# Decays of a gated recurrence as running products of f instead of exponentials of summed logarithms, in a two-layer float32 trunk on one core

## The chip, the cores and the metric

The kernel runs on one core of a Trainium2 chip. A core has a matrix engine (TensorE, PE in the profile, with PEld for its loading of stationary operands), a vector engine (VectorE, DVE), a scalar engine (ScalarE, ACT), GpSimd (POOL) and SyncE (SP), which here only issues transfers. Each engine works through its own queue in order and waits there for semaphores of the others. The metric is the device time of one execution in microseconds (us), as a median over runs.

## The reference

```python
for l in range(DEPTH):                                   # two layers, 256 tokens, width 1024, all float32
    x = x + 0.5 * swiglu(rms_norm(x, ffn1_norm[l]), ffn1_w_gate[l], ffn1_w_up[l], ffn1_w_down[l])
    h = rms_norm(x, mix_norm[l])
    if l < N_A_LAYERS:                                   # layer 0: gated linear recurrence, 6 heads of 128
        f = lb[l] + (1.0 - lb[l]) * sigmoid(f_raw)       # f_raw, q_raw, i_raw, g_raw: columns of h @ w_in_a
        q = silu(q_raw)
        o = hgrn2_recurrence(q, 1.0 - f, i_raw, log(f))  # S_t = diag(f_t) S_{t-1} + k_t v_t^T, o_t = S_t^T q_t
        main = rms_norm(o, hgrn_o_gain[l]) * silu(g_raw)
    else:                                                # layer 1: forgetting attention, 12 heads of 64
        main = forgetting_attention(q, k_sh, v_sh, cum_log_f) * sigmoid(gate)
    x = x + concatenate([main, memory_attention(...)]) @ w_out[l]
    x = x + 0.5 * swiglu(rms_norm(x, ffn2_norm[l]), ffn2_w_gate[l], ffn2_w_up[l], ffn2_w_down[l])
```

In the recurrence the score of query t against key s (s not after t) is the sum over 128 channels of q[t] k[s] times the product of f over the tokens after s up to t.

## The kernel before

**Weights and projections.** All weights stream from memory as 341 pieces of 128x1024. For each, ACT rounds the piece to a short float32 form (`wh`, line 359) and DVE forms the rest (`wl = raw - wh`, line 360); activations are split the same way into `xh` and `xl`. A product is three matmuls, wh*xh, wh*xl and wl*xh, each 128x128 by 256 columns, in a helper at line 294. Such matmuls are called dense here. Five pieces have room, so ACT and DVE can work up to five ahead of PE. A projection chunk is two pieces, 48 dense matmuls.

**Order.** PE runs in the order in which the program issues to it. A small planner, `Flow`, decides that order while the program is built: the dense matmuls advance a planned clock, and side work stands in generators (chains) that `yield` either a planned delay from the table `DELAY` or a condition. After every third dense matmul the planner lets one chain that is ready by the planned clock go on. Nothing on the chip follows these delays: if the data are late, PE waits at that place in its queue. The other engines' queues are ordered by a scheduler.

**PSUM.** The eight banks are `mm` (3, dense results), `lb` (2, scores and logits), `tb` (2, transposes) and `ob` (1, products with v).

**Mixer of layer 0.** `ORDER_A` gives the order of 15 chunks after the first FFN: f, q, i, g are the projections of three pairs of heads each, M the keys and values of the memory tokens, m the memory query. A chunk of f comes out with tokens on partitions; ACT takes the sigmoid, DVE applies the lower bound (rows `lv`, `ov`, spread over the partitions by two matmuls in `constants`) and clamps, PE transposes f to channels on partitions (12 transposes), and DVE forms k = 1 - f. `recurrence` then takes logarithms, splits them, and `decays` gets all products of f by matmuls of 512 columns with a constant 0/1 matrix `amat`: 8 for each of 6 heads, each pair of which ends in an exponential on ACT (line 929). There are seven levels (block lengths 64, 32, 16, 8, 4, 2, 1) and one slot for the step from the first 128 tokens to the second. `level_products` multiplies them by q or k, 128 columns at a time, on DVE and partly on POOL (lines 941, 944). `scores(hg)` multiplies per level on PE and copies the masked parts into a `unit` tile with predicated copies on DVE (line 971). `hgrn_out(hg)` multiplies by v into the one `ob` bank, squares on ACT (line 1031), forms 1/sqrt on DVE with eleven small instructions (lines 425 to 430), waits for the gate chunk g, multiplies (line 1041), transposes on PE after a planned delay `o0`, `o1` or `o2`, and `put` splits the result into the operand of the output projection (lines 665, 666).

**Elsewhere.** The memory attention of layer 0 starts when the scores of pair `MEM_WHEN` exist. `pair_out` is the product with v of the memory attention and of layer 1's attention (`fox_pair`, six pairs); it takes `ob` as soon as it is free, divides on DVE (lines 683, 691) and transposes. The output projection `project_out` takes four groups of rows in a given order, and finishes the chains of a group before it.

Of the kernel before, what the change touches and what calls it, by code (L numbers as in the profile page):

```python
# [27 lines left out]
TINY = 2.0 ** -62  # L28
# [5 lines left out]
         "f": 4.5, "ln": 7.5, "x": 7.5, "x2": 2.4, "norm_k": 8.2, "norm_b": 7.0, "norm_q": 8.75,  # L34
# [3 lines left out]
         "o0": 2.4, "o1": 1.42, "o2": 6.4, "mh": 1.0, "mp": 0.5, "cc": 74.5}  # L38
# [7 lines left out]
MEM_WHEN = 2  # L46
MEM_PRIO = 2
ORDER_A = "fffqMqqmiMiiggg"
# [46 lines left out]
def _stream(a):  # L95
# [4 lines left out]
    chunks = {"f": _as(wa[:, 768:1536]), "q": _ws(wa[:, 0:768]), "m": _as(wa[:, 3072:3328]),  # L100
# [21 lines left out]
def _shape_consts():  # L122

    u = np.arange(P)[:, None]
    t = np.arange(P)[None, :]

    def level(m):
        base = (t // (2 * m)) * (2 * m) + m
        up = (t % (2 * m)) >= m
        return np.where(up, (u >= base) & (u <= t), (u > t) & (u < base))  # L130

    suffix = u > t
    prefix = u <= t
    a = [level(m) for m in LEVELS]
    blocks = [a[0:4], a[4:7] + [suffix], a[4:7] + [prefix]]
    amat = np.concatenate([np.concatenate(b, axis=1) for b in blocks], axis=1).astype(np.float32)
    masks = np.zeros((P, len(LEVELS), 64), np.float32)
    for i, m in enumerate(LEVELS):
        s = np.arange(P)
        blk, low = s // (2 * m), (s % (2 * m)) < m  # L140
        cb = np.repeat(np.arange(64 // m), m)
        masks[:, i, :] = (blk[:, None] == cb[None, :]) & low[:, None]
    neg = np.where(np.arange(P)[None, :] > np.arange(P)[:, None], -1e30, 0.0).astype(np.float32)
    return amat, masks, neg, np.eye(P, dtype=np.float32)
# [6 lines left out]
def _layout(a):  # L151
    amat, masks, neg, ident = _shape_consts()
# [14 lines left out]
        "amat": amat,  # L167
# [72 lines left out]
def trunk(ctx: ExitStack, tc: tile.TileContext, d: dict, out: bass.AP):  # L240
# [8 lines left out]

    live = {"mm": 0, "lb": 0, "ob": 0, "hid": 0, "b6": 0}  # L250
# [9 lines left out]
    def free(tag, n=1):  # L260
        live[tag] -= n

    def has(tag, n=1):
        return lambda: live[tag] + n <= room[tag]

# [403 lines left out]
    def pair_out(pTs, v, heads, terms, mixed, k, gate=None, before=None):  # L669
        yield has("ob")  # L670
# [154 lines left out]
    con = {}  # L825

    lc = sb.tile([P, 12], F32, tag="lc", name="lc")
# [11 lines left out]
    def constants():  # L839
        yield lambda: softmax_c.done  # L840
        raw, araw = b6(), b6()
        with tc.issue_after(last_load[0]):
            for name, c, n in (("masks", 0, NM), ("wf", NM, KT * 12)):
                nc.sync.dma_start(out=raw[:, c:c + n], in_=d[name])
            nc.sync.dma_start(out=neg[:, P:T], in_=d["neg"])
            nc.sync.dma_start(out=fbias, in_=d["fbias"])
            nc.sync.dma_start(out=araw[:, 0:1536], in_=d["amat"])
# [5 lines left out]
        amat = con["amat"] = b6(F32R)  # L853
        G.tensor_copy(out=amat[:, 0:1536], in_=araw[:, 0:1536])
        free("b6", 2)

        G.tensor_tensor(out=lc[:, 6:12], in0=lc[:, 0:6], in1=lc[:, 0:6], op=ALU.subtract)
        lbt, lbd = b6(), b6()
        lv, ov = con["lv"], con["ov"] = lbt[:, 0:MAIN], lbt[:, MAIN:2 * MAIN]
        G.tensor_tensor(out=lbd[:, 0:MAIN].rearrange("p (h c) -> p h c", h=6),  # L860
                        in0=ident.unsqueeze(1).broadcast_to([P, 6, P]),
                        in1=lc[:, 6:12].unsqueeze(2).broadcast_to([P, 6, P]), op=ALU.mult)
        yield DELAY["const"]
        for i in range(2):
            b = bank("tb")
            mm(b[:, 0:384], ones, lbd[:, i * 384:(i + 1) * 384], True, True)
            S.copy(out=lv[:, i * 384:(i + 1) * 384], in_=b[:, 0:384])
        G.tensor_scalar(out=ov, in0=lv, scalar1=-1.0, scalar2=1.0, op0=ALU.mult, op1=ALU.add)
        free("b6")
# [10 lines left out]
    lv, ov = con["lv"], con["ov"]  # L880
# [3 lines left out]
    f, t1, t2, kT = b6(), b6(), b6(), b6()  # L884
    fv, t1v, t2v = tv(f), tv(t1), tv(t2)

    def f_chunk(c, o):
        yield lambda: st1.r is not None
        sl = slice(c * T, (c + 1) * T)
        for tt in range(2):  # L890
            S.activation(out=fv[:, tt, sl], in_=o[:, tt * T:(tt + 1) * T], func=AF.Sigmoid, scale=st1.r[:, tt:tt + 1])
        free("mm")
        fs = fv[:, :, sl]
        V.tensor_tensor(out=fs, in0=fs, in1=ov[:, sl].unsqueeze(1).broadcast_to([P, 2, T]), op=ALU.mult)
        V.tensor_tensor(out=fs, in0=fs, in1=lv[:, sl].unsqueeze(1).broadcast_to([P, 2, T]), op=ALU.add)
        V.tensor_scalar(out=t1v[:, :, sl], in0=fs, scalar1=TINY, scalar2=None, op0=ALU.max)
        V.tensor_scalar(out=t2v[:, :, sl], in0=fs, scalar1=1.0 / TINY, scalar2=TINY, op0=ALU.mult, op1=ALU.max)
        if c == 2:
            free("b6")
        yield DELAY["f"]  # L900
        b = bank("tb")
        for hh in range(2):
            for tt in range(2):
                transpose(b[:, (2 * hh + tt) * P:(2 * hh + tt + 1) * P], fv[:, tt, (2 * c + hh) * P:(2 * c + hh + 1) * P])
        V.tensor_scalar(out=kT[:, c * 512:(c + 1) * 512], in0=b, scalar1=-1.0, scalar2=1.0,
                        op0=ALU.mult, op1=ALU.add)
        if c == 2:
            free("b6")
# [4 lines left out]
    got = {"q": False, "x": set(), "s": set(), "v": set(), "g": set()}  # L913
    ss = [None] * 3
    box = con

    def decays(hg):

        for h in (2 * hg, 2 * hg + 1):
            e = [hid(), hid()]  # L920
            es[h] = [t.rearrange("p (t l c) -> p t l c", t=2, l=4) for t in e]
            for half in range(2):
                for tt in range(2):
                    b = bank("lb")
                    i = 0 if half == 0 else 1 + tt
                    ab = box["amat"][:, i * 512:(i + 1) * 512]
                    mm(b, box["lfh"][:, tt, h * P:(h + 1) * P], ab, True, False)
                    mm(b, box["lfl"][:, tt, h * P:(h + 1) * P], ab, False, True)
                    S.activation(out=e[half][:, tt * 512:(tt + 1) * 512], in_=b, func=AF.Exp)
                    yield DELAY["e%d" % hg]  # L930

    def level_products(hg):

        for h in (2 * hg, 2 * hg + 1):
            qh, kh = qT[:, h * T:(h + 1) * T], kT[:, h * T:(h + 1) * T]
            for i, m in enumerate(LEVELS):
                ev = es[h][i // 4][:, :, i % 4, :].rearrange("p t (n w m) -> p t n w m", w=2, m=m)
                for w, src in ((1, qh), (0, kh)):
                    sv = src.rearrange("p (t n w m) -> p t n w m", t=2, w=2, m=m)
                    eng = G if (w == 0 and i >= 2) else V  # L940
                    eng.tensor_tensor(out=ev[:, :, :, w, :], in0=ev[:, :, :, w, :], in1=sv[:, :, :, w, :], op=ALU.mult)
            for tt, src in ((0, kh), (1, qh)):
                e8 = es[h][1][:, tt, 3, :]
                V.tensor_tensor(out=e8, in0=e8, in1=src[:, tt * P:(tt + 1) * P], op=ALU.mult)

    def scores(hg):
# [9 lines left out]
        for i0 in range(0, len(LEVELS), 2):  # L956
            b = bank("lb").rearrange("p (a j c) -> p a j c", a=2, j=4)
            pair = range(i0, min(i0 + 2, len(LEVELS)))
            for i in reversed(pair):
                m = LEVELS[i]  # L960
                for j in range(4):
                    e = es[2 * hg + j // 2][i // 4][:, j % 2, i % 4, :]
# [12 lines left out]
        for hh in range(2):  # L975
            e = es[2 * hg + hh][1]
            mm(b[:, hh * P:(hh + 1) * P], e[:, 0, 3, :], e[:, 1, 3, :], hh == 0, True)
# [4 lines left out]
    def recurrence():  # L982
        yield lambda: len(fc) == 3 and all(c.done for c in fc)
        S.activation(out=t1[:, 0:W2], in_=t1[:, 0:W2], func=AF.Ln)
        S.activation(out=t2[:, 0:W2], in_=t2[:, 0:W2], func=AF.Ln)
        V.scalar_tensor_tensor(out=t1[:, 0:W2], in0=t2[:, 0:W2], scalar=0.0, in1=t1[:, 0:W2], op0=ALU.min, op1=ALU.add)
        free("b6")
        yield has("b6", 2)
        lfh, lfl = b6(F32R), b6(F32R)
        lfhv, lflv = tv(lfh), tv(lfl)  # L990
        box["lfh"], box["lfl"] = lfhv, lflv
        for tt in range(2):
            S.copy(out=lfhv[:, tt, :], in_=t1v[:, tt, :])
            V.tensor_tensor(out=lflv[:, tt, :], in0=t1v[:, tt, :], in1=lfhv[:, tt, :].bitcast(F32), op=ALU.subtract)
        free("b6")
        yield DELAY["ln"]
        yield lambda: live["hid"] + 8 <= room["hid"]
        yield from decays(0)
        yield from decays(1)
        yield lambda: got["q"]  # L1000
        level_products(0)
        level_products(1)
        yield DELAY["x"]
        yield from scores(0)
        yield lambda: live["hid"] + 4 <= room["hid"]
        yield from decays(2)
        free("b6", 3)
        level_products(2)
        yield from scores(1)
        yield DELAY["x2"]  # L1010
        yield from scores(2)
        free("b6", 2)

# [291 lines left out]
```

## Time and profile before

| what | value |
|---|---|
| median of 3 runs | 1088.21 us (1088.13 to 1088.75) |
| the profiled execution | 1089.6 us, its span 1087.8 us |
| mean granted TensorE clock | 0.998 of full speed |
| PE busy | 1066.6 us, 98% of the span |
| DVE, ACT, POOL busy | 740.9, 542.5, 123.1 us |
| chain that ended last, by engine | PE 91%, DVE 3%, ACT 2% |

The span is the time between the first and the last instruction of the profiled execution; the 1.8 us beside it lie around it. PE's busy time is modelled and overlaps from one matmul to the next, so "98%" does not say that PE runs at its peak; how often PE stood still is read from its waits.

### The profile page before, as it was taken

The page shows a single profiled execution, that of the slowest core. Times are in us where ns is not written, and L with a number is a line of the kernel's source. Part 1 is how long each engine was busy: PE and PEld are TensorE (multiplying, and loading weights), DVE is VectorE, ACT ScalarE, POOL GpSimd, SP SyncE. Part 2 cuts the span into 40 slices and gives each one's busy share as a digit, 9 for nine tenths or more (in the row PEclk, how much of TensorE's full clock was granted, in tenths as well). Part 3 has the DMA queues.
Part 4 walks back from the last instruction along what each step waited for, and adds up shares of the span by engine and source line. Part 5 has one row for each costly group of instructions (what it writes and reads, how often), then busy time and mean ns, then how long its engine had stood idle before and what let it go on. Part 6 is the DMA issues. An engine that isn't in the chain of part 4 may idle for free.

```text
span 1087.8 us, 21647 instructions
## 1 busy us (share of the span) xinstructions
PE 1066.6 (98%) x8882; PEld 1056.7 (97%) x8882; DVE 740.9 (68%) x1329; ACT 542.5 (50%) x814; POOL 123.1 (11%) x160
## 2 busy tenths in 40 slices
PE   6899999999999999999999999999999999999998
PEld 5899999999999999999999999999999999999998
DVE  7866665688877676666669666666685577666652
ACT  6554444468544455444544745444467445454431
POOL 7100201202240220000210000002200031000000
PEclk9999999999999999999999999999999999999999
DMA  6555655554322365555554565555543245555561
GB/s 229 196 188 193 212 192 179 195 190 159 134 97 77 111 191 183 189 181 193 175 184 165 166 204 185 185 194 174 187 144 117 97 150 182 194 181 188 194 194 59
DMA packets 52587, 185.12 MB, mean 170 GB/s; under 512 B 6256, under 2 KB 7688, under 8 KB 52488
## 3 DMA queue, kind: packets, MB, share of 16 engines
q1 hardware_dynamic: 52344, 183.70, 50.8%
q8 instruction: 69, 1.13, 0.4%
q14 instruction: 30, 0.25, 0.1%
q10 hardware_dynamic: 144, 0.04, 0.0%
HBM read 182.64 MB, written 1.05 MB: 169 GB/s over the span
## 4 chain that ended last, share of the span: by engine, by line
PE 91%; DVE 3%; ACT 2%; DMA 1%; issue 1%; POOL 0%; ACTq 0%; DVEq 0%
PE mm L294 61%; PE lb L294 26%; PE ob L294 2%; PE tb L298 1%; DVE wl L360 1%; ACT wh L359 1%; DVE xl L441 1%; PE tb L294 1%; DMA raw<-in_wts 0%; DMA hid<-in_memT 0%; DMA cols<-in_cols 0%; ACT xh L440 0%; ACT hid L645 0%; POOL ss L458 0%; DVE small L428 0%
## 5 line engine op out<-in xcount | busy, mean ns | idle before, releaser
L360 DVE TENSOR_TENSOR wl<-raw,wh 128x1024 fp32r<-128x1024 f32 (+1 forms) x341 | 426.1, 1251 | 195.3 <-ACT wh L359 193.7
L359 ACT CAST wh<-raw 128x1024 fp32r<-128x1024 f32 (+1 forms) x341 | 356.6, 1046 | 310.1 <-PE mm L294 156.6
L294 PE MATMUL mm<-hid,wh 128*128 128x256 f32 x1408 | 253.6, 283 | 0.0
L294 PE MATMUL mm<-xh,wl 128*128 128x256 f32 x880 | 246.5, 280 | 3.2 <-DVE wl L360 3.2
L294 PE MATMUL mm<-xh,wh 128*128 128x256 f32 x880 | 248.8, 283 | 0.1
L294 PE MATMUL mm<-xl,wh 128*128 128x256 f32 x880 | 246.3, 280 | 0.1
L294 PEld LDWEIGHTS mm<-hid,wh 128*128 128x128 f32 x1408 | 219.6, 192 | 0.0
L294 PE MATMUL mm<-hid,wl 128*128 128x256 f32 x704 | 199.2, 283 | 0.0
L294 PE MATMUL lb<-xh,wl 128*128 128x256 f32 x704 | 196.8, 280 | 1.8 <-DVE wl L360 1.8
L294 PE MATMUL lb<-xh,wh 128*128 128x256 f32 x704 | 198.0, 281 | 0.0
L294 PE MATMUL lb<-xl,wh 128*128 128x256 f32 x704 | 196.7, 279 | 0.0
L294 PEld LDWEIGHTS mm<-xh,wl 128*128 128x128 f32 x880 | 165.9, 189 | 3.6 <-DVE wl L360 3.6
L294 PEld LDWEIGHTS mm<-xl,wh 128*128 128x128 f32 x880 | 165.9, 189 | 0.8 <-DVE xl L663 0.3
L294 PEld LDWEIGHTS mm<-xh,wh 128*128 128x128 f32 x880 | 165.8, 188 | 0.8 <-ACT xh L662 0.3
L294 PE MATMUL mm<-wh,xh 128*128 128x256 f32 x432 | 131.8, 305 | 6.6 <-ACT wh L359 6.6
L294 PEld LDWEIGHTS mm<-hid,wl 128*128 128x128 f32 x704 | 135.2, 192 | 0.0
L294 PEld LDWEIGHTS lb<-xh,wl 128*128 128x128 f32 x704 | 132.4, 188 | 2.2 <-DVE wl L360 2.2
L294 PEld LDWEIGHTS lb<-xh,wh 128*128 128x128 f32 x704 | 132.5, 188 | 0.1
L294 PEld LDWEIGHTS lb<-xl,wh 128*128 128x128 f32 x704 | 132.5, 188 | 0.1
L294 PE MATMUL mm<-wl,xh 128*128 128x256 f32 x432 | 122.8, 284 | 1.5 <-DVE wl L360 1.3
L294 PE MATMUL mm<-wh,xl 128*128 128x256 f32 x432 | 122.4, 283 | 0.0
L294 PEld LDWEIGHTS mm<-wh,xh 128*128 128x128 f32 x432 | 82.8, 192 | 8.1 <-ACT wh L359 6.6
(180 smaller groups left out, 1063.3 us busy)
## 6 DMA issues: line engine op xcount, KB each, us to landing
raw<-in_wts SPq DMA_DIRECT2D x339, 512.0 KB, 3.3
hid<-in_memT SPq DMA_DIRECT2D x4, 256.0 KB, 4.8
xT<-in_xT SPq DMA_DIRECT2D x2, 512.0 KB, 6.6
hid<-in_memT SPq DMA_DIRECT2D x2, 512.0 KB, 5.8
out_xT<-xT SPq DMA_DIRECT2D x8, 128.0 KB, 1.9
b<-in_amat SPq DMA_DIRECT2D x1, 768.0 KB, 4.6
raw<-in_wts SPq DMA_DIRECT2D x2, 256.0 KB, 4.7
b<-in_masks SPq DMA_DIRECT2D x1, 224.0 KB
```

What stands on the lines that cost most here:

```text
L294: nc.tensor.matmul(out=out, lhsT=lhsT, rhs=rhs, start=start, stop=stop, skip_group_check=True)
L298: nc.tensor.transpose(out=out, in_=in_, identity=ident)
L359: S.copy(out=wh[:, c], in_=raw[:, c])
L360: V.tensor_tensor(out=wl[:, c], in0=raw[:, c], in1=wh[:, c].bitcast(F32), op=ALU.subtract)
L441: V.scalar_tensor_tensor(out=xl[:, k, :], in0=src, scalar=col, in1=xh[:, k, :].bitcast(F32), op0=ALU.mult, op1=ALU.subtract)
```

## The change

The recurrence no longer takes logarithms. f is projected with channels on partitions (rows of the diff with `_ws`), so it needs no transposes, and its lower bound is one number per partition. For each pair of heads, `running` works from block length 1 up to 64: `f1` and `ks` are updated in place so that they hold the product of f from the start of a block to each token, and k times the product from a token to the end of a block; each level's operands (`e0` from ks, `e1` from f times q) go to a slot of a `hid` tile. ACT copies `e0`, DVE does the products on 256 columns. The matrix `amat`, its transfer, the clamps, the splits and POOL's share are gone. f and q chunks take turns, the three pairs are chains of their own, one after the other, and the memory attention starts after the scores of pair 1. `hgrn_out` now waits for its gate chunk and a planned 2.5 before its product with v, not between the small instructions and the gating; and `hgrn_out` and `pair_out` take `ob` only 3.0 planned after it was freed (`rested`). `o0`, `o1` and `o2` stay.

```diff
-         "f": 4.5, "ln": 7.5, "x": 7.5, "x2": 2.4, "norm_k": 8.2, "norm_b": 7.0, "norm_q": 8.75,
+         "f": 4.5, "ln": 7.5, "x": 2.5, "x2": 2.5, "norm_k": 8.2, "norm_b": 7.0, "norm_q": 8.75,
-         "o0": 2.4, "o1": 1.42, "o2": 6.4, "mh": 1.0, "mp": 0.5, "cc": 74.5}
+         "lv": 1.7, "tq": 0.8, "ob": 3.0, "copy_g": 2.5, "o0": 2.4, "o1": 1.42, "o2": 6.4, "mh": 1.0, "mp": 0.5, "cc": 74.5}
...
-MEM_WHEN = 2
+MEM_WHEN = 1
-ORDER_A = "fffqMqqmiMiiggg"
+ORDER_A = "fqfqMMmfqigigig"
...
-    chunks = {"f": _as(wa[:, 768:1536]), "q": _ws(wa[:, 0:768]), "m": _as(wa[:, 3072:3328]),
+    chunks = {"f": _ws(wa[:, 768:1536]), "q": _ws(wa[:, 0:768]), "m": _as(wa[:, 3072:3328]),
...
         live[tag] -= n
+        freed[tag] = flow.now
     def has(tag, n=1):
         return lambda: live[tag] + n <= room[tag]
+
+    def rested():
+        return live["ob"] == 0 and flow.now >= freed["ob"] + DELAY["ob"]
     def hid():
         take("hid")
...
     def pair_out(pTs, v, heads, terms, mixed, k, gate=None, before=None):
-        yield has("ob")
+        yield rested
         take("ob")
...
+        raw = b6()
+        free("b6")
+        G.tensor_scalar(out=lc[:, 12:18], in0=lc[:, 6:12], scalar1=-1.0, scalar2=1.0, op0=ALU.mult, op1=ALU.add)
...
     def f_chunk(c, o):
...
+        yield lambda: st1.rB is not None
+        sl = slice(c * 512, (c + 1) * 512)
+        V.tensor_tensor(out=f[:, sl].rearrange("p (h t) -> p h t", h=2), in0=o.rearrange("p (h t) -> p h t", h=2),
+                        in1=st1.rB.unsqueeze(1).broadcast_to([P, 2, T]), op=ALU.mult)
         free("mm")
...
+        S.activation(out=f[:, sl], in_=f[:, sl], func=AF.Sigmoid)
+        for h in (2 * c, 2 * c + 1):
+            V.tensor_scalar(out=f[:, h * T:(h + 1) * T], in0=f[:, h * T:(h + 1) * T], scalar1=ov[:, h:h + 1],
+                            scalar2=lv[:, h:h + 1], op0=ALU.mult, op1=ALU.add)
+        V.tensor_scalar(out=kT[:, sl], in0=f[:, sl], scalar1=-1.0, scalar2=1.0, op0=ALU.mult, op1=ALU.add)
     fc = []
     es = {}
...
+    got = {"q": set(), "x": set(), "s": set(), "v": set(), "g": set()}
     ss = [None] * 3
...
+    box = {}
+    def slot(hg, i):
+        return es[hg][i // 2][:, (i % 2) * 512:(i % 2 + 1) * 512]
+    def halves(ap, m):
+        v = ap.rearrange("p (n w m) -> p n w m", w=2, m=m)
+        return v[:, :, 0, :], v[:, :, 1, :]
+    def running(hg):
+        es[hg] = [hid() for _ in range(4)]
+        sl = slice(hg * 512, (hg + 1) * 512)
+        fp, ks, k, q = f[:, sl], box["ks"][:, sl], kT[:, sl], qT[:, sl]
+        for i in reversed(range(len(LEVELS))):
+            m = LEVELS[i]
+            n = 256 // m
+            src = k if m == 1 else ks
+            (f0, f1), (s0, s1) = halves(fp, m), halves(src, m)
+            e0, e1 = halves(slot(hg, i), m)
+            S.copy(out=e0, in_=s0)
+            V.tensor_tensor(out=e1, in0=f1, in1=halves(q, m)[1], op=ALU.mult)
+            low, up = f0[:, :, m - 1:m].broadcast_to([P, n, m]), f1[:, :, m - 1:m].broadcast_to([P, n, m])
+            if m < 64:
+                k0, k1 = halves(ks, m)
+                V.tensor_tensor(out=k0, in0=s0, in1=up, op=ALU.mult)
+                if m == 1:
+                    S.copy(out=k1, in_=s1)
+                V.tensor_tensor(out=f1, in0=f1, in1=low, op=ALU.mult)
+            else:
+                x = slot(hg, 7).rearrange("p (h t w m) -> p h t w m", h=2, t=2, w=2)
+                h4 = lambda ap: ap.rearrange("p (h t) m -> p h t m", h=2)
+                f0, f1, s0, s1, e1, q0, q1 = map(h4, (f0, f1, s0, s1, e1, *halves(q, m)))
+                one = lambda ap, t: ap[:, :, t, 63:64].broadcast_to([P, 2, 64])
+                V.tensor_tensor(out=x[:, :, 0, 0, :], in0=s0[:, :, 0, :], in1=one(f1, 0), op=ALU.mult)
+                S.copy(out=x[:, :, 0, 1, :], in_=s1[:, :, 0, :])
+                V.tensor_tensor(out=x[:, :, 1, 0, :], in0=f0[:, :, 1, :], in1=q0[:, :, 1, :], op=ALU.mult)
+                V.tensor_tensor(out=x[:, :, 1, 1, :], in0=e1[:, :, 1, :], in1=one(f0, 1), op=ALU.mult)
+            yield DELAY["lv"]
     def scores(hg):
         s = unit().rearrange("p (j c) -> p j c", j=6)
...
+    def recurrence(hg):
+        yield lambda: hg in got["q"] and len(fc) > hg and fc[hg].done and (hg == 0 or hg - 1 in got["x"])
+        yield lambda: live["hid"] + 4 <= room["hid"]
+        if hg == 0:
+            take_ks()
+        yield from running(hg)
+        got["x"].add(hg)
         yield DELAY["x"]
...
+        yield from scores(hg)
+        if hg == 2:
+            free("b6", 4)
+    def take_ks():
+        box["ks"] = b6()
     def hgrn_out(hg):
...
+        yield lambda: hg in got["s"] and hg in got["v"] and hg in got["g"]
+        yield DELAY["copy_g"]
+        yield lambda: rested() and live["hid"] < room["hid"]
         take("ob")
...
-        yield lambda: hg in got["g"]
...
-    rec = flow.spawn(recurrence(), prio=PRIO["rec"])
+    for hg in range(3):
+        flow.spawn(recurrence(hg), prio=PRIO["rec"])
...
-        if c == 2:
-            flow.until(lambda: "lfl" in box and has("b6")())
-            sq = b6()
-            S.activation(out=sq[:, 0:W2], in_=qT[:, 0:W2], func=AF.Tanh)
-            for i in range(3):
-                sl = slice(i * 512, (i + 1) * 512)
-                V.scalar_tensor_tensor(out=qT[:, sl], in0=sq[:, sl], scalar=1.0, in1=qT[:, sl], op0=ALU.add, op1=ALU.mult)
-            free("b6")
-            got["q"] = True
+        flow.until(has("b6"))
+        sq, sl = b6()[:, 0:512], slice(c * 512, (c + 1) * 512)
+        S.activation(out=sq, in_=qT[:, sl], func=AF.Tanh)
+        V.scalar_tensor_tensor(out=qT[:, sl], in0=sq, scalar=1.0, in1=qT[:, sl], op0=ALU.add, op1=ALU.mult)
+        free("b6")
+        got["q"].add(c)
...
-            fc.append(flow.spawn(f_chunk(c, as_chunk(hx)), prio=PRIO["f"]))
+            fc.append(flow.spawn(f_chunk(c, ws_chunk(hx)), prio=PRIO["f"]))
```

**Order on DVE, in the recurrence of pair 0.** In the kernel before, these are products of one level after the other, with the decay of a head in `hid` and k or q in a `b` tile:

```order
L941 TENSOR_TENSOR hid<-hid,b_2983 128x2x2x32
L941 TENSOR_TENSOR hid<-hid,b_2983 128x2x4x16
L941 TENSOR_TENSOR hid<-hid,b_2983 128x2x8x8
L941 TENSOR_TENSOR hid<-hid,b_2983 128x2x16x4
L941 TENSOR_TENSOR hid<-hid,b_2983 128x2x32x2
```

In the changed kernel a level is three rows: line 902 is `e1` (f times q), line 906 the update of ks (`b_2843`), line 909 that of f (`b_2637`); line 1033 ends q's silu of pair 1:

```order
L902 TENSOR_TENSOR hid<-b_2637,b_2792 128x32x8
L906 TENSOR_TENSOR b_2843<-b_2843,b_2637 128x32x8
L1033 SCALAR_TENSOR_TENSOR b_2792<-b_2982,b_2792 128x512
L909 TENSOR_TENSOR b_2637<-b_2637 128x32x8
L350 TENSOR_TENSOR wl<-raw,wh 128x1024
L902 TENSOR_TENSOR hid<-b_2637,b_2792 128x16x16
L906 TENSOR_TENSOR b_2843<-b_2843,b_2637 128x16x16
```

What moved: a level's products now follow from the level before it, stand in the same queue as the splits of the weights (line 350 now), and the update of ks overwrites what ACT copies.

**Order on PE, at the product with v of pair 1 in layer 0.** Before, 45 rows (39 of them dense) stand between this product and the transposes of its result, since the gate lies between; in the changed kernel the product and the transposes (line 288 now) have 15 dense matmuls between them, of which the first and last three are shown:

```order
L284 MATMUL ob<-b_3656,unit 128x128 x6
L284 MATMUL mm<-wh,xh 128x256
L284 MATMUL mm<-wl,xh 128x256
L284 MATMUL mm<-wh,xl 128x256
...
L284 MATMUL mm<-wh,xh 128x256
L284 MATMUL mm<-wl,xh 128x256
L284 MATMUL mm<-wh,xl 128x256
L288 MATMUL tb<-ident,hid 128x128 x4
```

What moved: squares, small instructions and gating now all lie between these two places.

**Order on PE, at the last pairs of layer 1's attention.** Before, the products of two pairs (`ob`) have nine dense matmuls and a transpose between them:

```order
L294 MATMUL ob<-b_9465,unit 128x65 x6
L294 MATMUL mm<-xh,wh 128x256
L294 MATMUL mm<-xl,wh 128x256
L294 MATMUL mm<-xh,wl 128x256
L298 MATMUL tb<-ident,tmp 128x128 x2
...
L294 MATMUL ob<-b_9465,unit 128x65 x6
```

In the changed kernel the products of pairs 3, 4 and 5 stand behind one another:

```order
L288 MATMUL tb<-ident,tmp 128x128 x2
L284 MATMUL ob<-b_9326,b_9330 128x65 x6
L284 MATMUL ob<-b_9326,unit 128x65 x12
L288 MATMUL tb<-ident,tmp 128x128 x2
L284 MATMUL mm<-xh,wh 128x256
```

What moved: nothing stands between three products that share one bank.

## Rows read from the trace of the kernel before

**Rows 1.** The page's first section: busy time, share, instructions by engine.
```profile
PE 1066.6 (98%) x8882; PEld 1056.7 (97%) x8882; DVE 740.9 (68%) x1329; ACT 542.5 (50%) x814; POOL 123.1 (11%) x160
```

**Rows 2.** Mixer: start:end, length, busy PE, PEld, DVE, ACT, POOL, clock, DMA.
```profile
220.94:393.91 172.97, 170.36 (x1401) 165.91 (x1399) 136.74 (x302) 94.26 (x158) 42.32 (x54) 1.00 0.37 124
```

**Rows 3.** Waits from 200 to 395: who for whom, us, times, longest.
```profile
PE tb L298 <- DVE tmp L687: 1.3, 1, 1.3
...
PE lb L294 <- ACT hid L649: 0.5, 1, 0.5
...
PE tb L298 <- DVE b L895: 0.3, 1, 0.3
```

**Rows 4.** Chain that ended last, output projection's last operand: start, us, what.
```profile
365.66 0.38 ACT xh L662
366.07 0.43 DVE xl L663
...
366.55 19.59 PE mm L294 x164
```

**Rows 5.** The same chain, decays: first and last of 24 such rows.
```profile
256.90 0.47 PE lb L294 x2
...
314.50 0.46 PE lb L294 x2
```

**Rows 6.** The same chain: lower bound; a dense run; f's transposes, one of three.
```profile
125.41 1.29 PE tb L294 x4
...
235.56 5.67 PE mm L294 x48
241.23 0.44 PE tb L298 x4
```

**Rows 7.** DVE in time: start, us, instruction, shapes, count, wait before it.
```profile
246.61 0.76 DVE L1066 TENSOR_TENSOR b<-mm,rBh 128x256 f32<-128x256 f32 x2 [0.35 <-PE mm L294]
...
250.68 2.36 DVE L360 TENSOR_TENSOR wl<-raw,wh 128x1024 fp32r<-128x1024 f32 x2
...
285.85 1.90 DVE L941 TENSOR_TENSOR hid<-hid,b 128x128 f32<-128x128 f32 x9
```

**Rows 8.** PE in time: the sum of squares ahead of the mixer.
```profile
226.38 0.60 PE L294 MATMUL tb<-onesm,ss 128*128 128x1 f32 x4 [0.28 <-POOL ss L458]
```

**Rows 9.** The chain in pair 0's scores: one level, and two levels.
```profile
290.00 0.89 PE lb L294 x8
...
291.95 1.26 PE lb L294 x16
```

**Rows 10.** ACT in time: first square after pair 1's product with v.
```profile
330.39 0.28 ACT L1031 ACTIVATE hid<-ob 128x128 f32<-128x128 f32 x1 [0.31 <-PE ob L294]
```

**Rows 11.** DVE in time: gating of pair 0; first and last small instruction.
```profile
325.83 0.86 DVE L1041 SCALAR_TENSOR_TENSOR hid<-ob,small,b 128x128 f32<-128x128 f32 x3
...
331.57 0.17 DVE L1033 TENSOR_SCALAR small<-small 128x4 f32<-128x4 f32 x1 [0.23 <-ACT hid L1031]
...
334.42 0.16 DVE L1036 TENSOR_TENSOR small<-small,r 128x4 f32<-128x4 f32 x1
```

**Rows 12.** The chain in layer 1: two products with v, gating between.
```profile
856.32 1.30 PE ob L294 x12
...
857.91 0.86 DVE tmp L691 x4
...
858.91 1.52 PE ob L294 x12
```

**Rows 13.** Two stretches as in rows 2; the clock stands third from the end.
```profile
34.00:38.00 4.00, 4.00 (x24) 4.00 (x25) 3.34 (x17) 0.92 (x3) 0.20 (x1) 0.66 0.63 198
...
364.00:366.00 2.00, 0.76 (x5) 0.59 (x5) 1.03 (x4) 0.62 (x2) 0.00 (x0) 1.00 0.37 66
```

**Rows 14.** The chain at the start, in the first of these stretches.
```profile
33.82 2.50 PE mm L294 x10
```

**Rows 15.** The page's groups: ACT's casts of weights, number, busy us, mean ns.
```profile
L359 ACT CAST wh<-raw 128x1024 fp32r<-128x1024 f32 (+1 forms) x341 | 356.6, 1046 | 310.1 <-PE mm L294 156.6
```

## Prediction of the changed kernel's time

> **What bounds the kernel now.** I read the page's busy times first [rows 1]: PE is busy for 98% of the span, DVE for 68%, ACT for half, POOL for a tenth. The reader is to see that PE sets the time and that DVE is the next one. The change lies in the mixer of layer 0, so I took that stretch [rows 2]: 173.0 us, PE almost always busy and DVE for 137 of them. How long PE stood still there tells whether saved PE work counts. The view of waits gives it [rows 3]: 1.3, 0.5 and 0.3 us; and the chain shows one more [rows 4]: after the last transposes ACT and DVE split the operand until 366.5, and PE starts in earnest at 366.55, of which I count 0.7 as lost. That is 2.8 in 173. So in this stretch a matmul that goes is time saved, and a new wait of PE is time lost, one for one.
>
> **What is removed.** The decays stand in the chain as 24 rows of two matmuls with 512 columns, 0.466 each [rows 5]: 11.2. The transposes of f are three rows of 0.44, the spreading of the lower bound is one of 1.29 [rows 6]: 2.6. Together 13.8. f's chunks are 48 dense matmuls in either form, 0.118 each (48 in 5.67, [rows 6]). Logarithms, exponentials, POOL's products and the transfer of the 0/1 matrix I cost at nothing: PE's dense matmuls covered them. Without that cover their price would be that of the waits below.
>
> **What is added on DVE.** A level of a pair is now three products of 128x256, on operands with strides and repeats that the trace doesn't show. Bounds: 0.20 apart (nine of 128x128 in 1.90) and 0.60 (half of a split of 128x1024, two of which take 2.36); the nearest is 128x256 from PSUM, two in 0.76, so 0.34 to 0.38 [rows 7]. I take 0.34. For three pairs that is about 20 us where the old logs, clamps and products also took some 30: DVE's total hardly moves. What moves is when PE asks for the results.
>
> **Wait 1, scores of pair 0.** The statistic's matmuls start at 226.38 [rows 8] and 54 dense ones follow, then the spreading of the norm: pair 1's f begins at 233.7. Then come 48 of f, 48 of q, 63 of M, k times q (0.89, [rows 9]) and 9 dense: PE wants levels 64 and 32 at 254.5. DVE is free for f and q from about 234.5, and by its order has until level 64: six splits (6.8), 26 products of 128x256 (8.8), four of 512 (2.8), ten cheaper ones (1.7), 20.1 in all. That ends at 254.6; behind tanh and sigmoid, which stand on ACT between casts of weights, I add 1.7: 256.3. PE can do the half of its first row (1.26, [rows 9]) that needs level 32 alone, so it waits 1.2. Behind it DVE has seven predicated copies, twelve products of pair 1, two splits and the norm of the memory keys, about 11 us, against 9.1 of PE until its last row: 1.8 more. Wait 1 is 3.0; bounds 0 (no waits behind ACT, products at 0.20) and 6 (products at 0.60 would make it far longer, but nothing comes near that). Queued behind DVE's level products are the splits; five pieces of room keep PE supplied meanwhile. Pair 1's levels I find ready 1.2 before PE asks: 0.
>
> **Waits 2 to 4, products with v.** This is the part that I think decides. Formerly the gate lay between the small instructions and the gating, and PE had 45 rows to do. Now everything runs in one piece while `o0`, `o1`, `o2` are what they were. Its length: the first square [rows 10] starts with the product's end; DVE's first small instruction comes 1.2 later; thirteen small ones, 0.20 apart, take 2.6 (331.57 to 334.6, with a longer one among them); gating four blocks takes 1.15 (three in 0.86) [rows 11]; 0.15 until PE sees it. That is 5.1. The four transposes wait for one block each, so 0.3 of their time runs beside it. For pair 1 PE has 15 dense matmuls (1.85): wait 2.9. For pair 0 it has 15 dense, k times q and the first row of pair 2's scores (4.0), but DVE has a product (0.6) and two predicated copies (0.9, a little over the 0.38 of a product from PSUM each) in between: wait 2.2. For pair 2 it has 42 dense (5.05) against 5.1 and one split (1.1): 0.9; and as pair 2 is now the last operand of the output projection, its split on ACT and DVE (0.38 and 0.43 for half as many columns, [rows 4]) costs 1.5: together 2.4. Bounds for the three: 4, if the small ones overlap more, and 9.
>
> **Wait 5, memory attention.** In both kernels the third head's logits wait for the first head's exponentials (0.5, [rows 3]). DVE's reductions now stand behind a split that waits for its cast: 1.0; bounds 0 and 2.
>
> **Layer 1.** `rested` changes only PE's order there. Two products with v that share the bank are 1.3 apart, from the first one's end at 857.6 to 858.91, while DVE gates [rows 12]; six dense matmuls (0.7) lay in that gap, so 0.6 was lost. Now pairs 3, 4 and 5 follow with nothing between: two gaps of 1.3, and pair 3's operand is split behind pair 5's gating, 0.8: 3.4, thus 2.8 more. Bounds 1.5 and 3.5.
>
> **The sum.** Mixer: 3.0 + 2.2 + 2.9 + 2.4 + 1.0 = 11.5 of waits for 2.8, so 8.7 more. -13.8 + 8.7 + 2.8 = -2.3. The profiled execution took 1089.6 (span 1087.8 and 1.8 around it): 1087.3. The median of the runs is 1.4 below the profiled execution: **1085.9**. By the bounds, mixer waits of 4 to 17 and layer 1 of 1.5 to 3.5 more, it lies between 1077.1 and 1092.1.
>
> **A rule against it.** New waits of 2 to 3 us could also lower the clock. [...]
>
> **Rivals.**
> A, the waits stay hidden. If DVE keeps up in the mixer and the new waits equal the old, only layer 1 gives back: 1089.6 - 13.8 + 2.8 - 1.4 = 1077.2. For it: DVE idled for 36 of the 173 us [rows 2], and wait 1 hangs on 1.7 us that I guessed. Against it: the 15 dense matmuls behind pair 1's product are in the order, and 5.1 against 1.85 isn't a close call.
> B, slower: the update of ks waits for ACT. It overwrites what ACT copies to `e0`, and ACT has casts of 1.05 (mean, [rows 15]) in the same queue; three lie among pair 0's copies and five among pair 1's. If each comes just ahead of a copy that DVE wants, pair 0's scores are 3.1 later and pair 1's 5.2 less its 1.2 of slack, 4.0: 1085.9 + 7.1 = 1093.0. It decides the sign from 2.3 on, and passes 0.2% from 4.5, about four of the eight casts. For it: PE asks for a cast's buffer and for a copy at about the same time. Against it: by the order most casts end before the level that they precede.
> C, the clock falls behind three of the waits, and ten matmuls of each cost 1.3 more, as at the start: 1085.9 + 4.0 = 1089.9.
>
> **Chances.** Measurements of this kernel tell about 0.2% (2.2 us) from no change, so faster means under 1086.0 and slower over 1090.4. The forecast's own case, 1083 to 1089, gets 0.55; half of it is under 1086.0, half is the same. A 0.18, B 0.20, C 0.05, other mishaps 0.02. Faster 0.27 + 0.18 = 0.45; same 0.28 + 0.05 = 0.33; slower 0.22. The range takes A's time as its lower end and stops short of B's worst: 1077 to 1092.
>
> **What would show it.** No matmuls of 512 columns and no logarithm in the mixer, its stretch about 4 us shorter (12.5 less work, plus the waits), and the first FFN 1.3 shorter. PE's waits in the mixer should stand at the transposes of `hid` behind the three products with v (DVE's gating as releaser, 2 to 3 us each for pairs 0 and 1) and at `lb<-hid` of pair 0 (1 to 3). In layer 1 two gaps of 1.3 between `ob` rows. Wrong would be: no wait at those transposes (A), level products on DVE that idle for ACT's copies by more than 4 us (B), or a granted clock under 1.00 in the mixer (C).

## The result, and the profile after

The changed kernel took 1098.47 us (median of 4 runs, 1097.03 to 1100.14) beside 1088.48 for the one before: a ratio of 1.0081 on record, 95% interval 1.0068 to 1.0093, so 0.8% slower (the two medians alone give 1.0092). Ratios below are those on record. The forecast was 1085.9 with a range up to 1092.

The page of the changed kernel, busy times:

```profile
PE 1063.5 (97%) x8818; PEld 1054.7 (96%) x8818; DVE 734.9 (67%) x1323; ACT 531.2 (48%) x809; POOL 99.0 (9%) x128
```

Against [rows 1], PE has 64 instructions fewer but only 3.1 us less of busy time. The matmuls that went were worth 13.8 [rows 5] [rows 6]. That is the first hint: those that are left took longer. Four stretches of the changed kernel follow the whole mixer of layer 0 (columns as in [rows 2]):

```profile
218.34:395.70 177.36, 166.77 (x1341) 163.24 (x1339) 131.18 (x296) 83.91 (x154) 23.06 (x24) 0.95 0.34 120
223.00:226.50 3.50, 3.50 (x17) 3.50 (x18) 2.36 (x3) 1.05 (x1) 1.49 (x3) 0.51 0.43 150
325.30:335.80 10.50, 10.50 (x54) 10.50 (x53) 3.92 (x6) 2.18 (x4) 0.00 (x0) 0.51 0.15 50
349.30:353.00 3.70, 3.21 (x15) 2.99 (x16) 1.92 (x6) 1.93 (x4) 0.00 (x0) 0.54 0.00 0
878.30:888.80 10.50, 8.74 (x38) 8.20 (x39) 2.75 (x14) 0.75 (x2) 0.00 (x0) 0.51 0.13 48
```

The third number from the end is the granted clock. Before, it was 1.00 over the whole mixer; now there are three stretches at 0.51 to 0.54 in the mixer and one at 0.51 in layer 1. What PE loses in one I estimate from these rows as its busy time by what is missing of the clock: 1.7, 5.1, 1.5 and 4.3, together 12.6.

PE's waits in the mixer, to set beside [rows 3] (us in total, times, longest):

```profile
PE tb L288 <- DVE hid L1001: 4.8, 3, 2.4
...
PE lb L284 <- ACT hid L639: 1.2, 1, 1.2
...
PE lb L284 <- DVE unit L947: 1.1, 1, 1.1
...
PE mm L284 <- DVE xl L431: 1.0, 1, 1.0
...
PE lb L284 <- DVE hid L902: 0.8, 1, 0.8
...
PE mm L284 <- ACT xh L655: 0.8, 1, 0.8
...
PE mm L284 <- ACT xh L430: 0.6, 1, 0.6
```

With 0.4 for `xl L656` they make 10.7; the prediction had 11.5. Of the 10.7, the 1.6 at lines 430 and 431 stand at the mixer's start, where none was forecast; the forecast waits came to 9.1. What followed a wait was not forecast. The chain behind the product with v of pair 0 (start, us, what):

```profile
318.13 1.15 ACT hid L992 x8
...
323.58 0.36 DVE hid L1001
...
324.08 1.01 PE tb L288 x4
325.09 0.36 PE mm L284 x3
325.45 2.93 PE lb L284 x16
328.38 2.03 PE mm L284 x9
```

Squares, small instructions and gating take from 318.1 to 324.0 and PE stands still for the last 1.9 of it. Then nine dense matmuls take 2.03 and 16 of the scores 2.93; the same rows take 1.12 and 1.62 in experiment 1. A wait of 1.9 was followed by some ten microseconds at a clock of 0.51, the row of 325.30 above.

The difference by stages, between the starts of the matmuls that spread a norm (end: from the last one to the end of the span):

| stage | before | after | difference |
|---|---|---|---|
| up to the mixer's first matmul | 221.0 | 218.3 | -2.6 |
| mixer, to the norm of the second FFN | 182.3 | 186.7 | +4.4 |
| to the norm of layer 1's first FFN | 184.1 | 184.1 | 0.0 |
| layer 1, to the norm of its second FFN | 326.9 | 334.9 | +8.0 |
| end | 173.5 | 172.5 | -0.9 |

The mixer should have lost 12.5 of PE work. It gained 10.7 - 2.8 = 7.9 of waits and 8.3 of slow clock: 3.7 of the 4.4. Layer 1 gained 3.5 of waits and 4.3 of slow clock: 7.8 of the 8.0.

### The profile page after: what moved, and what is told of

It is laid out like the page before. It is cut to its first block, busy times and chain, and to the rows that moved or that the text cites. A ratio compares the mean times of both kernels' runs of the same rounds, so it can differ in the third digit from the quotient of the medians.

```text
span 1096.7 us, 21458 instructions
## 1 busy us (share of the span) xinstructions
PE 1063.5 (97%) x8818; PEld 1054.7 (96%) x8818; DVE 734.9 (67%) x1323; ACT 531.2 (48%) x809; POOL 99.0 (9%) x128
## 4 chain that ended last, share of the span: by engine, by line
PE 72%; DVE 5%; ACT 2%; issue 1%; POOL 0%; DVEq 0%; ACTq 0%
PE mm L284 49%; PE lb L284 19%; PE ob L284 2%; DVE wl L350 1%; PE tb L288 1%; ACT wh L349 0%; PE tb L284 0%; ACT hid L635 0%; POOL ss L448 0%; ACT hid L992 0%; DVE b L909 0%; DVE hid L902 0%; DVE b L906 0%; DVE small L418 0%; DVE small L637 0%
## 5 line engine op out<-in xcount | busy, mean ns | idle before, releaser
L284 PE MATMUL mm<-xh,wh 128*128 128x256 f32 x928 | 264.4, 285 | 1.4 <-ACT xh L655 0.8
L284 PE MATMUL mm<-xh,wl 128*128 128x256 f32 x928 | 260.7, 281 | 3.2 <-DVE wl L350 3.2
L284 PE MATMUL mm<-xl,wh 128*128 128x256 f32 x928 | 260.9, 281 | 2.0 <-DVE xl L431 1.0
L284 PEld LDWEIGHTS mm<-xh,wl 128*128 128x128 f32 x928 | 175.8, 189 | 3.6 <-DVE wl L350 3.6
L284 PEld LDWEIGHTS mm<-xl,wh 128*128 128x128 f32 x928 | 175.9, 190 | 3.0 <-DVE xl L431 1.2
L284 PEld LDWEIGHTS mm<-xh,wh 128*128 128x128 f32 x928 | 175.8, 189 | 2.1 <-ACT xh L655 1.0
L284 PE MATMUL mm<-wh,xh 128*128 128x256 f32 x384 | 118.0, 307 | 6.6 <-ACT wh L349 6.6
L284 PE MATMUL mm<-wl,xh 128*128 128x256 f32 x384 | 110.4, 288 | 1.9 <-DVE wl L350 1.8
L284 PE MATMUL mm<-wh,xl 128*128 128x256 f32 x384 | 110.0, 286 | 0.0
L284 PEld LDWEIGHTS mm<-wh,xh 128*128 128x128 f32 x384 | 75.1, 195 | 7.2 <-ACT wh L349 6.6
```

The lines of the kernel that those rows point to most:

```text
L284: nc.tensor.matmul(out=out, lhsT=lhsT, rhs=rhs, start=start, stop=stop, skip_group_check=True)
```

## Experiments

Two theories. **Clock**: PE's standing still is what lowers its clock, and the work behind the wait pays as much again or more. **Waits**: the new waits cost what they last, and the clock falls for another reason, such as the many small matmuls of the scores. The runs were made in three groups, in which the kernel before took 1090.2, 1089.7 and 1091.3, so ratios to it are compared. By the intervals, a difference between two kernels is sure to about 2 us only; where the theories lie closer than that, or a total is spoilt by slow stretches elsewhere, the trace of the stage has to decide, and that is one execution.

**1. Work in place of idling, one place.** 22 matmuls of constants into the bank that the transposes then overwrite; nothing else moves on any engine.

```diff
         b2 = bank("tb")
+        if hg == 0:
+            for _ in range(22):
+                nc.tensor.matmul(out=b2[:, 0:P], lhsT=ident, rhs=ident, start=True, stop=True, ...)
         for j in range(4):
             transpose(b2[:, j * P:(j + 1) * P], y[:, j * P:(j + 1) * P])
```

> The changed kernel with 22 matmuls of 128x128 added in front of the transposes of pair 0 (constants times constants, into the transposes' own bank, which the transposes then overwrite). They take about 2.4 us by four in 0.44, as long as PE waits there, and nothing else moves. Clock theory (PE standing still is what lowers the granted clock): it stays at 1.00 from 324 to 336, where it was 0.50 for 10.4 us, so 5.2 less: 1093.3. Wait theory (the new waits cost what they last, and the clock falls for another reason, such as the small matmuls of the scores): the clock falls all the same, 1098.5. If the matmuls simply add their own time, 1100.9.

Measured: 1.0082 (1.0064 to 1.0101), no change in the total. The chain, and the stretch behind the filling:

```profile
324.60 4.91 PE tb L1010 x44
329.51 0.44 PE tb L288 x4
329.94 0.36 PE mm L284 x3
330.31 1.62 PE lb L284 x16
331.93 1.12 PE mm L284 x9
```

```profile
329.50:340.00 10.50, 10.50 (x95) 10.50 (x93) 5.88 (x8) 3.67 (x6) 0.00 (x0) 1.00 0.17 51
```

A filling matmul took 0.22, not 0.11, so the filling was 4.9 long where the wait was 1.9. Still the time from the product of pair 0 to that of pair 1 fell from 26.1 (318.1 to 344.2) to 23.9: the scores behind ran at 1.00, 16 of them in 1.62 and nine dense in 1.12. That speaks for the clock theory at this place. With the filling's real length, 3.0 more than the wait, the clock theory gives 1096.3 for the total and the wait theory 1101.5; the ratio times 1088.48 is 1097.4 (1095.4 to 1099.5). No gain shows in it, as this profiled execution (mean clock 0.991) ran slowly at 35 to 39, as the kernel before did [rows 13], and had another stretch at 0.50 from 369.5 to 373.5, behind pair 2's wait, which had left the clock at 1.00 in the changed kernel (366 to 376).

**2. All fillings.** 55 such matmuls at seven places where PE waits, 7 to 10 a place (5 at the last), again with nothing else moved.

> The changed kernel with 55 matmuls of constants added in PE's queue at the places where it stands still and the clock fell: 7 at the mixer's start, 10, 9 and 7 ahead of the transposes of pairs 0, 1 and 2, 8 ahead of the output projection's last rows, 9 and 5 ahead of the last two products with v of layer 1. Each takes 0.22 by 44 records in 4.91 in the run with 22 of them. They replace idling, no wait gets shorter, and no other instruction moves. Clock theory: no stretch at 0.50 in the mixer or in layer 1, so 8.3 + 4.3 less, perhaps 1 lost where a filling is longer than its wait: 1087. Wait theory: no gain, 1098.5 to 1100.

Measured: 1.0011 (1.0000 to 1.0022), 7.6 us less than the changed kernel by the ratios. The whole mixer, and layer 1 around the fall:

```profile
220.13:391.91 171.78, 167.24 (x1423) 164.81 (x1421) 131.77 (x296) 84.70 (x156) 23.10 (x24) 1.00 0.40 126
860.00:890.00 30.00, 28.56 (x241) 27.64 (x240) 17.61 (x46) 10.00 (x18) 3.36 (x5) 1.00 0.28 91
```

The waits theory allowed no gain. By stages the mixer took 5.6 less and layer 1 3.3 less than in the changed kernel, together 8.9 of the 12.6. Of the rest, about 2 us are filling that outlasts its wait: at pair 2 it takes 1.56 and 1.79 where the waits were 0.5 and 1.2, at pair 0 2.23 for 1.9. The clock is on record for every run, as a mean over the span: 0.997 to 1.000 in all ten runs of this kernel, 0.987 to 0.989 in all four of the changed one. The small matmuls of the scores are the same in both, so they alone don't lower it. More useless work on the bottleneck engine made the kernel faster.

**3. Transposes later.** `"o0": 2.4, "o1": 1.42` become 5.5 and 5.5.

> The changed kernel with o0 and o1 at 5.5, so that PE does 15 to 30 more dense matmuls between the products with v of pairs 0 and 1 and their transposes. Clock theory: both waits (2.4 and 2.0) go, and the clock falls of 10.4 and 3.5 us at half speed with them (5.2 and 1.7): 1087.2. Wait theory: the waits alone, 1094.1. Rival (the wait moves on to the next thing that DVE owes PE): 1098.

Measured: 0.9994 (0.9981 to 1.0006), 9.5 less than the changed kernel; by stages the mixer takes 9.4 less. PE waits for nothing at the transposes of pairs 0 and 1, and the clock holds:

```profile
318.00:350.00 32.00, 32.00 (x282) 31.86 (x281) 22.97 (x56) 14.29 (x34) 1.41 (x1) 1.00 0.41 132
```

The waits theory could give 4.4. Of the expected 11.3, up to 1.7 went to a stretch at 0.50 behind pair 2's wait, from 360.0 to 363.5. In layer 1, where nothing is changed, the slow stretch was longer in this execution (868.6 to 882.3), and the stage took 1.3 more, 336.2.

**4. No rest of the bank.** `rested` returns `live["ob"] == 0` alone.

> The changed kernel with the planned rest of the ob bank undone: products with v take the bank as soon as it is free, as before. Layer 1's second part took 7.0 more than before, of which 4.3 lie in a stretch of 10.5 us at a granted clock of 0.50. Clock theory: all 7.0 come back, no stretch at 0.50 there: 1091.5. Wait theory: only the 2.8 of waits that the prediction counted: 1095.7. The mixer of layer 0 stays as slow as it is.

Measured: 1.0043 (1.0028 to 1.0057). Layer 1 takes 327.0, as before, where the changed kernel took 334.9, and the whole stage reads:

```profile
590.53:917.49 326.96, 325.89 (x2737) 323.16 (x2735) 219.94 (x443) 170.29 (x260) 25.75 (x32) 1.00 0.51 164
```

All 8.0 came back there, of which 3.5 were waits. That is more than the wait theory allows. The ratios differ by 4.1 only, the two profiled executions by 5.7: in this one the mixer takes 1.2 more (187.9; the memory attention's product now waits 0.8 for its bank) and the end 1.0 more. The other 1.6 lie between executions.

**5. The same part alone in the kernel before.** Only `pair_out` of the kernel before waits for 3.0 planned.

> The kernel before with one part of the change alone: the product with v of the memory attention and of layer 1 takes the ob bank only 3.0 planned after it was freed. Clock theory: the same back-to-back products as in the changed kernel, so its 8.0 in layer 1, of which 4.3 are a stretch at a granted clock of 0.50: 1096. Wait theory: 2.8 to 3.5 more, 1091 to 1092.

Measured: 1.0058 (1.0042 to 1.0073), so 6.3 slower; layer 1 takes 334.9, the 8.0 of the changed kernel. The waits are the same two, and the clock behind them is 0.50 from 878 to 887:

```profile
PE ob L296 <- DVE tmp L693: 3.5, 2, 2.2
```

This run holds something else. At the mixer's end, where almost nothing is changed, it has the wait of the kernel before in [rows 3], 1.3 for the memory attention's result, and behind it this stretch:

```profile
365.42 0.41 PE L300 MATMUL tb<-ident,tmp 128*128 128x128 f32 x2 [1.34 <-DVE tmp L689]
```

```profile
365.20:368.90 3.70, 3.48 (x16) 3.21 (x17) 0.49 (x2) 0.37 (x1) 0.00 (x0) 0.57 0.45 142
```

The kernel before, with the same wait (1.3 in [rows 3]), read there:

```profile
364.00:368.00 4.00, 2.60 (x18) 2.23 (x19) 1.46 (x5) 0.66 (x2) 0.00 (x0) 1.00 0.43 131
```

The place of which [rows 13] had shown a clock of 1.00 stands at 0.57 here.

**6. First chunk of f block by block.**

```diff
+        if k_outer:                      # the first chunk of f only
+            ww = piece(), piece()
+            for k in range(KT):
+                for m in range(2):
+                    ws3(acc, acc.t[:, m * T:(m + 1) * T], ww[m], k, x, k, k == KT - 1)
```

> The changed kernel with the first chunk of f alone taken in another order: both halves of its channels for each of the eight column blocks of x, so that PE needs the last block after 42 matmuls, not after 21. Clock theory: the two waits at the mixer's start (0.6 and 1.0) go, and the 3.4 us at half clock behind them: 1.6 + 1.7 = 3.3 less, 1095.2. Wait theory: 1096.9. If the second half's piece is late instead: 1098.5.

Measured: 1.0050 (1.0032 to 1.0069), 3.4 less. In the changed kernel PE waited twice for the last block of x:

```profile
221.57 0.38 PE L284 MATMUL mm<-xh,wh 128*128 128x256 f32 x1 [0.59 <-ACT xh L430]
222.91 0.44 PE L284 MATMUL mm<-xl,wh 128*128 128x256 f32 x1 [0.96 <-DVE xl L431]
```

With the other order both are gone. One of 1.4 for POOL's sum of squares stands there instead, and the clock holds behind it; from the mixer's first matmul to the spreading of its norm it takes 13.4, not 15.3:

```profile
219.00:230.00 11.00, 9.58 (x82) 9.38 (x81) 10.28 (x22) 6.71 (x11) 3.35 (x4) 1.00 0.48 151
```

So 1.9 came back although PE stood still for about as long as before. In 8 to 11 below, which keep this order, the clock is 1.00 there as well (220 to 232). The other 1.5 don't lie there: the slow stretch behind pair 0 was shorter in this execution (0.50 from 324.9 to 328.3), though there was one behind pair 2 as well (0.50 from 366 to 369). The total alone does not tell the expected 1095.2 from 1096.9.

**7. The gate wait at its old place.** `yield lambda: hg in got["g"]` stands before the gating again, and the product with v waits for s and v and a planned 1.25 alone.

> The changed kernel with the wait for the gate chunk back at its old place, between the small instructions and the gating. Clock theory: the waits at the transposes of pairs 0 and 1 (2.4 and 2.0) and behind pair 2 (1.7) go, and with them 5.2 and 1.7 of clock: 13.0 less, 1085.5. Wait theory: 6.1 less, 1092.4. Rival (the earlier products push DVE's other work back, so that the memory attention or the scores wait instead): 1090 to 1095.

Measured: 1.0045 (1.0030 to 1.0059), mixer 182.3, 4.5 less than in the changed kernel: a third of the expected gain. The rival came true:

```profile
PE tb L288 <- DVE hid L1002: 6.4, 2, 5.1
```

The product of pair 0 now comes while DVE still has pair 2's running products; its small instructions stand behind them and between splits, and the transposes, still 2.4 planned behind the gate, wait 5.1. The clock was 0.50 from 321.8 to 328.6, so it fell within this wait. PE's waits in this mixer add up to 12.4, more than the changed kernel's 10.7, and still it is faster, since it holds one slow stretch and not three.

**8 to 11. What is left of the change without its waits.** Number 8 is 4, 6 and 7 together. Number 9 is 3, 4 and 6 together with `"copy_g": 0.3`. Numbers 10 and 11 alter 9 by `"lv": 2.2` and by `MEM_WHEN = 2`.

> Only the running products, the new projection and order of f and q are left of the change: gate wait at its old place, no planned rest of the ob bank, and the first chunk of f taken block by block. Clock theory: 13.0 + 7.0 + 3.3 less than the changed kernel, 1075.2. Wait theory: 6.1 + 2.8 + 1.6 less, 1088.0.

> The gate wait stays ahead of the product with v, but the planned 2.5 behind it becomes 0.3, o0 and o1 become 5.5, there is no rest of the ob bank, and the first chunk of f is taken block by block. Clock theory: as for the run with the gate wait undone, the waits of pairs 0 and 1 go, pair 2's is 2.2 earlier and goes too: 1075 to 1077. Wait theory: 1088.

> The fastest kernel so far (gate wait ahead of the product, 0.3 behind it, o0 and o1 at 5.5, no rest, first chunk of f block by block), with the planned time of a level, lv, at 2.2 in place of 1.7, so that all scores stand later on PE. If the wait for the running products of pair 0 (0.8) and the one for its predicated copies (1.1) are only a matter of being asked for too early, they go: 1.9 less, 0.987 of before. Rival: the scores and the memory attention now pile up at the mixer's end, and as much is lost there: 0.989 or more.

> The fastest kernel so far with the memory attention after the scores of pair 2, as before the change, not of pair 1. If its early start matters (its 1.2 of wait stands beside free PE work, and later it would stand ahead of the output projection), 1 to 3 slower: 0.990 to 0.992 of before. If it does not: 0.989.

| run | ratio to before (95%) | mixer | layer 1 |
|---|---|---|---|
| 8, gate late, no rest, block by block | 0.9912 (0.9894 to 0.9929) | 174.6 | 327.0 |
| 9, late transposes, no rest, block by block | 0.9889 (0.9872 to 0.9906) | 172.3 | 326.9 |
| 10, 9 with lv 2.2 | 0.9927 (0.9913 to 0.9942) | 178.3 | 326.9 |
| 11, 9 with the memory attention later | 0.9872 (0.9856 to 0.9889) | 172.2 | 326.9 |

All four beat both kernels, by 0.7 to 1.3% the one before. Times 1088.48, 8 took 1078.9 and 9 took 1076.4, nearer to the clock theory's 1075.2 and 1075 to 1077 than to the other's 1088. 11 does not differ clearly from 9: the intervals overlap and the mixers are the same length, so the early start of the memory attention is worth nothing that shows. In 8, the early product did not hurt as in 7, which was not looked into further. In 10 the waits for the running products and copies of pair 0 did go, but the memory attention's product with v now stood behind pair 0's gating, which still held the bank:

```profile
PE ob L284 <- DVE hid L1007: 3.9, 1, 3.9
```

```profile
309.00:323.50 14.50, 11.61 (x54) 11.62 (x55) 5.46 (x19) 1.04 (x1) 0.67 (x1) 0.53 0.12 43
```

Saving 1.9 of short waits bought one of 3.9 and a slow stretch of 13.7 us, as long as the longest elsewhere, which began within that wait (309.9). In 11 the mixer's waits are these, and its clock is 1.00 throughout:

```profile
PE lb L284 <- DVE unit L953: 1.1, 1, 1.1
PE tb L284 <- POOL ss L454: 0.7, 1, 0.7
PE lb L284 <- DVE hid L908: 0.7, 1, 0.7
PE mm L284 <- DVE xl L662: 0.4, 1, 0.4
PE lb L284 <- ACT hid L645: 0.4, 1, 0.4
PE tb L288 <- DVE xl L662: 0.4, 1, 0.4
PE tb L288 <- DVE hid L1007: 0.3, 1, 0.3
```

```profile
218.37:381.14 162.77, 158.60 (x1341) 155.58 (x1340) 131.54 (x296) 84.65 (x156) 23.13 (x24) 1.00 0.42 133
```

Against 172.97 for the same work before [rows 2]: 10.2 less, the 12.5 of PE work less 4.0 of waits where 2.8 were (3.1 with the 0.3 of [rows 8], which the prediction left out), to within 1.1 to 1.4.

## Why the prediction was wrong, step by step

**The failed step** is that the sum holds nothing for the clock in the mixer, and with it rival C's chance of 0.05 and its price of 1.3 a wait (the 2.50 of [rows 14] less ten dense matmuls at 0.118). I took one wait that left the clock at 1.00 [rows 13] as proof that none would lower it; in experiment 5 the clock fell at that very place. The other stretch of [rows 13], with its 0.66, I set aside, as it comes behind long waits at the kernel's start; but the last of them is no longer than the new waits that I forecast:

```profile
33.82 0.58 PE L294 MATMUL mm<-xh,wl 128*128 128x256 f32 x1 [2.53 <-DVE wl L360]
```

What the runs showed in place of nothing, and of 1.3 a wait: slow stretches at four places, which by the estimate above cost 1.5 to 5.1 us each and 12.6 together, 8.3 in the mixer and 4.3 in layer 1; without them the profiled execution's 1098.5 would be 1085.9. That this meets the forecast is partly luck: the start came out 2.6 faster, and only 1.3 of that is saved work; the rest goes with the slow stretch at 34 to 38, which this execution did not have (1.00 from 33 to 39); and in the mixer 2.4 of waits that were counted too long stand against 1.6 that were missed.

**What was removed.** Right: the mixer's 12.5 show in runs 9 and 11, and the spreading of the lower bound in the start, though single executions differ there by 1 to 2.

**DVE's products.** Right at 0.34 (the last two of these rows; the first is k = 1 - f):

```profile
242.81 0.34 DVE b L872
243.15 0.33 DVE hid L902
243.48 0.34 DVE b L906
```

**Wait 1** was 1.9 (0.8 and 1.1 at the two places named), not 3.0: DVE's last level was done at 256.2, as forecast, and the rest was counted too long. **Waits 2 to 4** were 1.9, 2.4 and 1.7, not 2.2, 2.9 and 2.4, and all at the places named. **Wait 5** was 1.2 for 1.0. **Missed** was 1.6 at the mixer's start: f by channels needs the last block of x after 21 matmuls, which I could have read from the order on PE. **Layer 1** gained 3.5 of waits, its upper bound, not 2.8, as the gating of pair 3 stood behind a split; its 4.3 of clock I did not count at all.

**Rivals.** A was right in its price: runs 8, 9 and 11, which hide the long waits, lie at 0.987 to 0.991, and A's 1077.2 is 0.990. In part that is chance, since A's price holds 2.8 for layer 1 that these runs don't pay. B fell: DVE waited for ACT's copies 1.0 in all. C came true, at 12.6 in place of its 4.0, and in layer 1 too: experiments 1, 2 and 3 take the wait away and leave the scores, and the clock is 1.00 at those places; experiment 5 brings the waits of layer 1 into the kernel before, and there it is 0.50. The traces show 0.50 behind the waits above, 1.00 again 3 to 14 us later with PE at work, and stretches of other lengths behind one and the same wait (3 to 10 us at pair 0's transposes).

## What to carry to other kernels

Where PE is the bound, price a new wait of PE of some 2 us at its length and the slow stretch that may follow (1.5 to 5.1 us here, by the estimate above), and look for the granted clock in the stretch behind a wait too, not only in the one that holds it: the 7.0 us that end with pair 0's wait in the changed kernel (318.1 to 325.1) stand at 1.00. A wait that leaves the clock at 1.00 in one execution is no proof for the next one: at the mixer's end it was 0.57 in experiment 5. When a producer's chain moves as one piece, move its consumer's planned time with it: two delays in a table turned 0.8% slower into no change, and three more small edits turned that into 1.1% faster (a fourth added nothing clear).

## What was not expected of the hardware

The length of a slow stretch had little to do with that of its wait: in the changed kernel about 10 us at 0.51 behind a wait of 1.87 (pair 0, scores and dense matmuls in turns, PE busy throughout), 3.4 at 0.54 behind one of 2.43 (pair 1, dense matmuls behind it). And the same wait was not always followed by a lower clock, nor for as long. Counted over the profiled executions in which a wait stands unaltered (us):

| waits of PE | executions | followed by a slow stretch |
|---|---|---|
| kernel's start, 2.5 | 13 | 8 |
| mixer's start, two, 1.6 to 2.6 in all | 5 | 4 |
| pair 0's scores 1.07, memory attention 1.22 | 9 | 0 |
| pair 0's transposes, 1.87 | 3 | 3, of about 10, 7 and 3 us |
| pair 1's transposes, 2.43 | 4 | 3 |
| behind pair 2, three, 1.5 to 1.7 in all | 5 | 4 |
| mixer's end, 1.34 (kernel before, experiment 5) | 2 | 1 |
| layer 1 with `rested`, 2.25 and 1.26 | 6 | 6, of 10 to 14 us |

So the experiments show a clock of 1.00 where the waits were taken out, not that every wait lowers it; what decides that is not shown here. Even the short stretches are worth up to 1.7 us each by the estimate above, so two single traces can differ by this and more without any edit.

The scatter from run to run goes with the clock as well. In 38 runs of the kernel before, made beside the experiments, the nine with a mean clock of 0.999 or more took 1088.7 us (median) and the eleven at 0.996 or less 1091.7. Why the stretch behind pair 0 lasted so long in the changed kernel is open.
